# Hybrid decoder block on one core: right-hand tiles moved by 32 bytes, stores and loads moved between the SP and ACT queues, first, FFN-entry and last steps reordered

## The chip, the cores and the metric

The kernel runs on one core of one Trainium2 chip. The metric is the device time of one execution in microseconds (us). Of the kernel before, three runs are known: 1540.65, 1542.43 and 1542.45 us, median 1542.43. One further execution was profiled; the views quoted below are of it.

The engines: PE (TensorE) multiplies matrices, DVE (VectorE) and ACT (ScalarE) work element by element, POOL (GpSimd) too, and SP issues DMAs. Each engine takes its own instructions in the order in which they stand in the program. A DMA is issued by SP or by ACT, and its issue is an instruction of that engine like any other: if it has to wait, whatever stands behind it waits too.

## The reference

One decoder layer, 1024 positions by 1024 channels, fp32. Two branches, stick-breaking attention (8 heads of 64) and an HGRN2 recurrence (4 heads of 128), are merged by sigmoid gates and projected; a SwiGLU FFN with 2816 hidden channels follows.

```python
proj = rms_norm(x, norm1_g) @ w_in          # 1024 -> 5632
q_sb, k_sb, v_sb, q_hg, f_hg, i_hg, g_hg, gate_sb, gate_hg = split_cols(proj, IN_SIZES)
y_sb = stick_breaking_attention(q, k, v) @ w_branch[:512]
y_hg = hgrn2_mixer(q_hg, f_hg, i_hg, g_hg, lb, norm_g) @ w_branch[512:]
mixed = jax.nn.sigmoid(gate_sb) * y_sb + jax.nn.sigmoid(gate_hg) * y_hg
h = x + mixed @ w_out
hn = rms_norm(h, norm2_g)
out = h + (jax.nn.silu(hn @ w_gate) * (hn @ w_up)) @ w_down
```

## The kernel before, in words

**Operands.** Everything is kept transposed: 128 channels on the partitions, positions along the row, in halves of 512 (`hs(h)`). Each fp32 operand is split into a rounded part and a rest (`split`, L233: a cast on ACT for the first, a subtraction on DVE for the second), and each product is three matmuls of 128x512: hi·hi, hi·lo, lo·hi (`mm3` L297, `prod` L911, and L1060 to L1064). In the profile's names a matmul is `out<-moving,stationary`.

**Stages.** (1) Up to about 700 us: the input projection, attention and HGRN2, written as a list of operations that a planner (`Plan`, L74) puts in an order at build time; in the profile all of these have the line L182. (2) 700 to 785: the branch outputs times `wb` (L794 to L818). (3) 785 to 880: `w_out`, the residual sum `xx`, its store to the scratch tensor `h_d` (L860), and the operands `fop` of the FFN (L832 to L887). (4) 880 to 1320: gate and up, eleven pairs p of row blocks, each as a Winograd product of 2x2 blocks with seven sub-products numbered 1 to 7 (`winograd`, L961); the seven right-hand sums of each activation pair go to the scratch tensor `act_d` (L1008, L1017), those of `wd` to `wd_d`. (5) From 1320: the down projection, seven sub-products o in the order 1, 2, 6, 7, 4, 5, 3, each eleven pairs p of one `ra` (weights) and one `rb` (activations) tile, four banks d of 128 output rows (L1035 to L1079).

**Start.** ACT's first instruction is the load of its function table (L205). SP issues `vt<-vec` and then, in the planner's order, the eight x tiles `aa<-xT` of the first half with four weight tiles `kb<-wi` between them (L451 to L461). POOL makes the `oh` of each `kb`, DVE its `ol`; ACT makes the `ah` of each x tile, DVE its `al`.

**Queues.** Apart from the 32 `sig_d` stores, all DMAs are issued by SP in program order, so a load stands behind the stores written ahead of it. In stage 3 a chunk is one (k, h) of 24 matmuls; SP's load of the next `xx` stands behind the store of the last one. At the passage from stage 4 to 5 SP has the five stores of the last `act_d`, the loads of the pairs p = 4 to 10 of o = 1, 14 loads of `hb<-h_d`, and then the loads of o = 2; two further `hb` loads stand ahead of the stores. Pairs p = 0 to 3 of o = 1 (`early`, L1038) are loaded into other pools ahead of that. ACT has the casts `ah<-ra`, `bh<-rb` in order of p, and behind those of o = 1 four copies `acc<-f`, which wait for PE to end o = 1.

**FFN entry.** `winograd(..., begin=channel_sums)` runs once, for p = 0: sub-products 1, 5 and 6 over k = 0 to 2, then their k = 3 (whose operands are the last that stage 3 makes), then `begin()`, which sums the channels of `rr` (the squares that POOL adds up at L870), and only then ACT's copy `p1<-x` and DVE's `c[:, 1] = y + p1`, for which sub-product 7 waits.

**Addresses.** Pools are laid out from the left end of a partition's memory or, with `side="right"`, from the right end. In the built program every tile that PE streams from a left-hand pool (`xn`, `mx`, the `bh` and `bl` of stage 5) starts at a multiple of 64 bytes. The tiles of the right-hand pools start 32 bytes past such a multiple: among them the moving operands of stage 2 (`oh`, `ol` of `opool`, L786), all `fh`, `fl` of stage 4 (`fpool`, L824), and `khl` of the attention scores.

Of the kernel before, what the change touches and what calls it, by code (L numbers as in the profile page):

```python
# [10 lines left out]
F32 = mybir.dt.float32  # L11
# [8 lines left out]
P = 128  # L20
# [9 lines left out]
FILL = ["GgGGaifq", "gGaGfiqGG", "gaGGGiqGfGG", "gGGG"]  # L30
# [172 lines left out]
def hybrid_block(ctx: ExitStack, tc, xT, wi, wb, wo, wg, wu, wd, vec, outT):  # L203
    nc = tc.nc
    nc.scalar.preload_act_table_set("natural_log_exp_and_others")  # L205

# [19 lines left out]
    nc.sync.dma_start(vt, vec)  # L226
# [17 lines left out]

    rst = ExitStack()
# [47 lines left out]

    def hs(h):
        return slice(h * HALF, (h + 1) * HALF)
# [25 lines left out]
    xn = a_set(xst.enter_context(tc.tile_pool(name="xnp", bufs=1)))  # L321
    pre = ExitStack()
# [22 lines left out]
    st1 = ExitStack()  # L345
# [3 lines left out]
    hgp = st1.enter_context(tc.tile_pool(name="hgp", bufs=1, reuse_waits="tile"))  # L349
# [211 lines left out]

    COL = {"q": 0, "k": 4, "v": 8, "hq": 12, "hf": 16, "hi": 20, "hg": 24, "G": 28}
# [182 lines left out]
    fill = [("q", 0), ("k", 0), ("v", 0), ("hf", 0), ("hq", 0), ("hi", 0)]  # L745
# [85 lines left out]
    with tc.tile_pool(name="wot", bufs=4, reuse_waits="tile") as ot_:  # L831
        seq = [0, 4, 1, 5, 2, 6, 3, 7]  # L832
        wq = [get_w(wo[seq.pop(0)])]
        for i in range(4):
# [14 lines left out]
            for e in range(2):  # L849
# [4 lines left out]
                for h in range(2):  # L854
# [5 lines left out]
                    nc.sync.dma_start(h_d[k][:, hs(h)], xx)  # L860
# [6 lines left out]
                    else:  # L867
                        sq = tmp("sq")
                        nc.scalar.activation(sq, xx, AF.Square)
                        nc.gpsimd.tensor_tensor(rr[h], rr[h], sq, op=ALU.add)  # L870
# [65 lines left out]
    with ExitStack() as sta:  # L936
# [24 lines left out]
        def winograd(a, c, begin=None):  # L961
# [3 lines left out]
            if begin:  # L965
                for ks in ((0, 1, 2), (3,)):
                    for o, bank in ((1, x), (5, z), (6, y)):
                        prod(bank, a[o], fop[o], True, ks)
                begin()
                nc.scalar.copy(p1, x)  # L970
# [8 lines left out]
            prod(x, a[2], fop[2], False)  # L979
# [9 lines left out]
        for p in range(NP):  # L989
# [18 lines left out]
            nc.sync.dma_start(act_d[p][:, :4 * HALF], c.rearrange("p b t -> p (b t)"))  # L1008
# [7 lines left out]
            for b, t in ((4, n7), (5, n6), (6, n5), (7, n4)):  # L1016
                nc.sync.dma_start(act_d[p][:, b * HALF:(b + 1) * HALF], t)  # L1017
# [15 lines left out]
          5: [(d + 4, 1) for d in range(4)], 3: [(d, 1) for d in range(4)]}  # L1033
    bank = [None] * 4
    for o in DOWN:  # L1035
        first = o in (1, 6, 5)
        for p in range(NP):
            early = o == 1 and p < 4  # L1038
            wp, tags = bp, btags = dB, ("ah", "al")
            btags = ("bh", "bl")  # L1040
            if early:

                rp = wpool if p < 2 else preB
                raw = rp.tile([P, 1024], F32, tag="w", bufs=2, name="w32")
                ra, rb = raw[:, :512], raw[:, 512:]
                if p < 3:
                    wp = bp = rp
                    tags = btags = ("oh", "ol") if p < 2 else ("ds", "ds")
            else:
                ra = dB.tile([P, HALF], F32, tag="ra", name="ra")  # L1050
                rb = dB.tile([P, HALF], F32, tag="rb", name="rb")
            nc.sync.dma_start(ra, LEFT[o](p))
            nc.sync.dma_start(rb, blk(act_d[p], RIGHT[o]))
            hi, lo = split(ra, wp, tags)
            bh, bl = split(rb, bp, btags)
            for d in range(4):
                if first and p == 0:
                    bank[d] = fb()
                ws = slice(d * P, (d + 1) * P)
                nc.tensor.matmul(bank[d], hi[:, ws], bh, start=first and p == 0, stop=False,  # L1060
                                 skip_group_check=True)
                nc.tensor.matmul(bank[d], hi[:, ws], bl, start=False, stop=False,  # L1062
                                 skip_group_check=True)
                nc.tensor.matmul(bank[d], lo[:, ws], bh, start=False, stop=p == NP - 1,  # L1064
                                 skip_group_check=True)
        if o == 1:
            for k, h in ([(d, 0) for d in range(4)] + [(d, 1) for d in range(8)]
                         + [(d, 0) for d in range(4, 8)]):
                nc.sync.dma_start(hb[k][:, hs(h)], h_d[k][:, hs(h)])
            for d in range(4):  # L1070
                nc.scalar.copy(acc1[d], bank[d])
            continue
        for d, (k, h) in enumerate(TO[o]):
            t = hb[k][:, hs(h)]
            if o in (6, 7, 4):
                nc.vector.tensor_tensor(t, t, acc1[d], op=ALU.add)
            nc.vector.tensor_tensor(t, bank[d], t, op=ALU.add)
            if o in (2, 4, 5, 3):
                nc.sync.dma_start(outT[k][:, hs(h)], t)  # L1079
# [48 lines left out]
```

## Time and profile before

| What | Number |
| --- | --- |
| median of three runs | 1542.43 us (1540.65 to 1542.45) |
| the profiled execution, its own time | 1541.46 us |
| its span, first to last instruction | 1539.7 us |
| mean granted TensorE clock | 0.997 |
| DMA traffic | 188.5 MB, 122 GB/s over the span |
| DMA queue of SP (q1) / of ACT (q10) | 178.8 MB / 8.4 MB |

How the views are read: in the view of the stretches, a row gives the stretch, its length, then for each engine busy time and, in parentheses, how many instructions touched the stretch, the granted clock, the share of time the 16 DMA engines were busy, and GB/s. In the waits, a row gives who waited for whom, the sum, how often, and the longest. In the timeline, a row gives start, duration, engine, line, operation, `out<-in`, how many were merged, and in brackets the engine's idle time before it and what ended it. A matmul's end in the trace is modelled, so the pitch of matmuls is taken from how many start in a stretch. The stage borders above are read from the timeline.

### The profile page before, as it was taken

What the parts mean: (1) busy time and instruction counts of PE and PEld (TensorE: products, weight loads), DVE (VectorE), ACT (ScalarE), POOL (GpSimd) and SP (SyncE); (2) the same over time, 40 slices, a digit from 0 to 9 for tenths busy, and PEclk for the clock granted to TensorE, in tenths of its full rate; (3) what the DMA queues carried; (4) which work ended last, traced back from release to release, by engine and by line L of the source; (5) the groups of instructions that cost most, each with busy time, mean ns of one, the idle gap of its engine ahead of it and who ended that gap; (6) DMA issues with size and microseconds to landing.
All of it is one profiled execution on the core that took longest, in us unless ns stands there. A gap on an engine that the chain in (4) does not pass through costs nothing.

```text
span 1539.7 us, 20478 instructions
## 1 busy us (share of the span) xinstructions
PE 1515.8 (98%) x7213; PEld 1242.1 (81%) x7213; DVE 1184.3 (77%) x2046; ACT 800.4 (52%) x1503; POOL 178.8 (12%) x202
## 2 busy tenths in 40 slices
PE   8999999999999999999999989999999999999999
PEld 6788888888888888888888868778778888778887
DVE  8899679988898768965567798888877777475553
ACT  7866778678768778454333352233333333254442
POOL 4211111111111101114412200000000000000000
PEclk9999999999999999999999999999999999999999
DMA  5111211111111121245334455666633332787672
GB/s 178 41 43 44 76 33 42 59 39 52 50 52 41 59 69 48 71 160 201 125 107 133 139 163 205 217 211 208 213 136 110 105 105 94 270 274 220 193 220 92
DMA packets 78407, 188.53 MB, mean 122 GB/s; under 512 B 9056, under 2 KB 11104, under 8 KB 76896
## 3 DMA queue, kind: packets, MB, share of 16 engines
q1 hardware_dynamic: 73696, 178.83, 35.5%
q10 hardware_dynamic: 4608, 8.39, 1.5%
q8 instruction: 57, 0.93, 0.3%
q14 instruction: 46, 0.38, 0.1%
HBM read 131.61 MB, written 55.57 MB: 122 GB/s over the span
## 4 chain that ended last, share of the span: by engine, by line
PE 73%; DVE 11%; DMA 6%; ACT 4%; issue 4%; POOL 1%; SPq 1%; DVEq 0%; POOLq 0%; ACTq 0%
PE f L916 25%; PE pj L182 23%; PE ms L182 8%; PE f L1062 4%; PE f L1064 4%; PE f L1060 4%; PE z L182 2%; DMA xx<-xT 2%; DVE ol L238 1%; ACT aa L182 1%; DMA rb<-act_d 1%; POOL s L805 1%; DMA s<-sig_d 1%; DVE aa L182 1%; DVE tail L182 1%
## 5 line engine op out<-in xcount | busy, mean ns | idle before, releaser
L182 PE MATMUL pj<-ah,oh 128*128 128x512 f32 x704 | 286.7, 407 | 2.0 <-POOL oh L182 2.0
L182 PE MATMUL pj<-ah,ol 128*128 128x512 f32 x704 | 277.3, 394 | 0.9 <-DVE ol L182 0.9
L182 PE MATMUL pj<-al,oh 128*128 128x512 f32 x704 | 276.0, 392 | 0.0
L916 PE MATMUL f<-fh,oh 128*128 128x512 f32 x616 | 244.0, 396 | 3.4 <-ACT p L970 1.7
L916 PE MATMUL f<-fl,oh 128*128 128x512 f32 x616 | 243.4, 395 | 0.7 <-DVE fl L846 0.7
L916 PE MATMUL f<-fh,ol 128*128 128x512 f32 x616 | 243.2, 395 | 0.6 <-DVE ol L238 0.6
L237 ACT CAST oh<-w 128x512 fp32r<-128x512 f32 x168 | 102.1, 620 | 175.2 <-PE f L916 137.9
L182 PEld LDWEIGHTS pj<-ah,ol 128*128 128x128 f32 x704 | 132.6, 188 | 31.6 <-DVE ol L182 2.1
L182 PEld LDWEIGHTS pj<-ah,oh 128*128 128x128 f32 x704 | 133.1, 189 | 25.3 <-POOL oh L182 2.9
L182 PEld LDWEIGHTS pj<-al,oh 128*128 128x128 f32 x704 | 133.2, 189 | 22.9 <-issue 0.5
L916 PEld LDWEIGHTS f<-fh,oh 128*128 128x128 f32 x616 | 115.4, 187 | 34.3 <-ACT p L970 2.1
L916 PEld LDWEIGHTS f<-fh,ol 128*128 128x128 f32 x616 | 115.4, 187 | 29.1 <-DVE ol L238 1.0
L916 PEld LDWEIGHTS f<-fl,oh 128*128 128x128 f32 x616 | 115.5, 187 | 29.0 <-DVE fl L846 1.0
L238 DVE TENSOR_TENSOR ol<-w,oh 128x512 fp32r<-128x512 f32 x168 | 114.7, 690 | 30.0 <-ACT oh L237 29.8
L1062 PE MATMUL f<-bl,ah 128*128 128x512 f32 x296 | 117.0, 395 | 1.3 <-DVE bl L238 1.3
L1060 PE MATMUL f<-bh,ah 128*128 128x512 f32 x296 | 114.6, 391 | 3.7 <-ACT bh L237 3.7
L182 DVE TENSOR_TENSOR_SCAN aa<-aa,ww 128x128 f32<-128x128 f32 (+3 forms) x96 | 92.3, 975 | 33.4 <-ACT aa L182 23.8
L182 POOL TENSOR_SCALAR oh<-w 128x512 fp32r<-128x512 f32 x84 | 70.9, 844 | 394.0 <-PE pj L182 348.6
L1064 PE MATMUL f<-bh,al 128*128 128x512 f32 x296 | 116.6, 394 | 0.0
L238 DVE TENSOR_TENSOR al<-ra,ah 128x512 fp32r<-128x512 f32 x73 | 50.4, 690 | 72.0 <-ACT ah L237 71.9
L237 ACT CAST ah<-ra 128x512 fp32r<-128x512 f32 x73 | 45.5, 623 | 101.8 <-PE f L1062 93.7
L182 ACT ACTIVATE aa<-aa 128x512 f32<-128x512 f32 (+3 forms) x128 | 69.1, 552 | 4.9 <-DVE aa L182 4.0
(273 smaller groups left out, 2996.7 us busy)
## 6 DMA issues: line engine op xcount, KB each, us to landing
w<-wi SPq DMA_DIRECT2D x42, 512.0 KB, 3.6
rb<-act_d SPq DMA_DIRECT2D x73, 256.0 KB, 4.1
w<-wg SPq DMA_DIRECT2D x22, 512.0 KB, 3.9
w<-wu SPq DMA_DIRECT2D x22, 512.0 KB, 4.1
w<-wd SPq DMA_DIRECT2D x22, 512.0 KB, 6.8
wd_d<-ds SPq DMA_DIRECT2D x44, 256.0 KB, 5.4
act_d<-c SPq DMA_DIRECT2D x11, 1024.0 KB, 3.9
act_d<-bs SPq DMA_DIRECT2D x44, 256.0 KB, 3.5
```

The lines of the kernel that those rows point to most:

```text
L182: fn(*[a.real() if isinstance(a, View) else a for a in args], **{k: v.real() if isinstance(v, View) else v for k, v in kw.items()})
L237: pin(nc.scalar.copy(hi, src))
L238: pin(nc.vector.tensor_tensor(lo, src, hi.bitcast(F32), op=ALU.subtract))
L805: nc.gpsimd.tensor_tensor(s[:, hs(h)], s[:, hs(h)], rr1[h], op=ALU.mult)
L916: nc.tensor.matmul(out, a[i][:, ws], bl[k][j], start=start and k == 0 and i + j == 0, stop=k == 3 and i == 1, skip_group_check=True)
L1060: nc.tensor.matmul(bank[d], hi[:, ws], bh, start=first and p == 0, stop=False, skip_group_check=True)
L1062: nc.tensor.matmul(bank[d], hi[:, ws], bl, start=False, stop=False, skip_group_check=True)
L1064: nc.tensor.matmul(bank[d], lo[:, ws], bh, start=False, stop=p == NP - 1, skip_group_check=True)
```

## The change

It has nine parts. (a) A tile `edge` of 32 bytes is put at the right end ahead of all right-hand pools; in the built program every right-hand tile then starts at a multiple of 64 bytes. (b) `vt` and the four `kb` tiles are loaded by ACT, ahead of its table load; SP loads x alone. The planner now sees the `kb` tiles as present from the start. (c) One filler projection G changes places in the planner's list. (d) The `h_d` stores of stage 3 are issued by ACT. (e) The 14 sums of `rr` go from POOL to DVE. (f) In the first Winograd product sub-product 1 and its copy `p1` come first, sub-product 2 moves ahead of the last k of sub-product 6. (g) The last pair's `act_d` stores are issued by ACT. (h) The `hb` loads are issued by ACT, two behind each pair p >= 3 of o = 1. (i) In the last sub-product the last three pairs are run bank by bank, so that each bank ends, is summed and stored ahead of the next.

```diff
-FILL = ["GgGGaifq", "gGaGfiqGG", "gaGGGiqGfGG", "gGGG"]
+FILL = ["GgGGaifq", "gGaGfiqGG", "gGaGGiqGfGG", "gGGG"]
...
-    nc.scalar.preload_act_table_set("natural_log_exp_and_others")
...
-    nc.sync.dma_start(vt, vec)
+    nc.scalar.dma_start(vt, vec)
...
+    edge = ctx.enter_context(tc.tile_pool(name="edge", bufs=1, side="right"))
+    nc.gpsimd.memset(edge.tile([P, 8], F32, name="edge"), 0.0)
     rst = ExitStack()
...
+    first_w = []
+    for i in range(2):
+        for n, v in fill_cols[:2]:
+            t = hgp.tile([P, HALF], F32, tag="kb", bufs=4, name="kb")
+            nc.scalar.dma_start(t, wi[COL[n] + v][:, hs(i)])
+            first_w.append(t)
+    nc.scalar.preload_act_table_set("natural_log_exp_and_others")
...
-                n, v = fill[u]
-                w = new("kb")
-                load(w, wi[COL[n] + v][:, hs(i)], 256)
-                ws[u].append(split_w(w))
+                t = first_w[2 * i + u]
+                plan.ring("kb", 4)
+                ws[u].append(split_w(Buf("kb", lambda t=t: t)))
...
-                    nc.sync.dma_start(h_d[k][:, hs(h)], xx)
+                    nc.scalar.dma_start(h_d[k][:, hs(h)], xx)
...
-                        nc.gpsimd.tensor_tensor(rr[h], rr[h], sq, op=ALU.add)
+                        nc.vector.tensor_tensor(rr[h], rr[h], sq, op=ALU.add)
...
             if begin:
-                for ks in ((0, 1, 2), (3,)):
-                    for o, bank in ((1, x), (5, z), (6, y)):
-                        prod(bank, a[o], fop[o], True, ks)
+                prod(x, a[1], fop[1], True)
+                nc.scalar.copy(p1, x)
+                prod(z, a[5], fop[5], True)
+                prod(y, a[6], fop[6], True, range(3))
+                prod(x, a[2], fop[2], False)
+                prod(y, a[6], fop[6], True, (3,))
                 begin()
-                nc.scalar.copy(p1, x)
                 nc.vector.tensor_tensor(c[:, 1], y, p1, op=ALU.add)
...
             prod(y, a[7], fop[7], False)
-            prod(x, a[2], fop[2], False)
+            if not begin:
+                prod(x, a[2], fop[2], False)
...
-            nc.sync.dma_start(act_d[p][:, :4 * HALF], c.rearrange("p b t -> p (b t)"))
+            store = nc.scalar.dma_start if p == NP - 1 else nc.sync.dma_start
+            store(act_d[p][:, :4 * HALF], c.rearrange("p b t -> p (b t)"))
...
-                nc.sync.dma_start(act_d[p][:, b * HALF:(b + 1) * HALF], t)
+                store(act_d[p][:, b * HALF:(b + 1) * HALF], t)
...
+            if o == 1 and p >= 3:
+                for k, h in HB[2 * p - 6:2 * p - 4]:
+                    nc.scalar.dma_start(hb[k][:, hs(h)], h_d[k][:, hs(h)])
...
+    rest = [(p, operands(o, p)) for p in range(NP - LAST, NP)]
+    for d in range(4):
+        for p, ops in rest:
+            step(d, p, ops, False)
+        finish(o, d)
```

The functions `operands`, `step` and `finish` of the last piece hold the former loop bodies: the two loads with their splits, the three matmuls of one bank, and the sum into `hb` with its store.

**DVE at the start of the program.** `al` is the rest of an x tile, `ol` that of a weight tile, `tail` a sum of squares, `mk` a mask. Before:

```order
L292 TENSOR_SCALAR nomlb<-omlb 128x4
L182 SCALAR_TENSOR_TENSOR al_152<-aa,vt,ah_151 128x512
L182 TENSOR_TENSOR ol<-kb,oh 128x512
L182 SCALAR_TENSOR_TENSOR al_154<-aa,vt,ah_153 128x512
L182 TENSOR_TENSOR tail<-tail,ww 128x512
L182 TENSOR_TENSOR ol<-kb,oh 128x512
L182 SCALAR_TENSOR_TENSOR al_156<-aa,vt,ah_155 128x512
```

At the same place of the program as changed:

```order
L293 TENSOR_SCALAR nomlb<-omlb 128x4
L182 TENSOR_TENSOR ol<-kb,oh 128x512 x4
L182 SCALAR_TENSOR_TENSOR al_156<-aa,vt,ah_155 128x512
L182 COPY mk_242<-tmp 128x256
L182 SCALAR_TENSOR_TENSOR al_158<-aa,vt,ah_157 128x512
L182 SCALAR_TENSOR_TENSOR al_160<-aa,vt,ah_159 128x512
```

All four `ol<-kb` have moved ahead of the first `al`; PE's second matmul reads that `al` in both programs.

**ACT and SP at the passage from stage 4 to 5.** `w_12667` and `w_12672` are the raw tile of an early pair, `hb` the residual. ACT before:

```order
L237 CAST oh<-w_12303 128x512
L237 CAST oh<-w_12301 128x512
L237 CAST ah<-w_12667 128x512
L237 CAST bh<-w_12667 128x512
L237 CAST ah<-ra 128x512
L237 CAST bh<-rb 128x512
```

ACT of the program as changed:

```order
L235 CAST oh<-w_12308 128x512
L235 CAST oh<-w_12306 128x512
L1093 DMA hb_12587<-h_d_144 128x512
L1093 DMA hb_12588<-h_d_145 128x512
L1021 DMA act_d_132<-c 128x2048
L1030 DMA act_d_132<-bs 128x512 x4
L235 CAST ah<-w_12672 128x512
L235 CAST bh<-w_12672 128x512
L1093 DMA hb_12589<-h_d_146 128x512
L235 CAST ah<-ra 128x512
L235 CAST bh<-rb 128x512
```

SP before, from the loads of the early pairs on:

```order
L1052 DMA w_12621<-wd 128x512
L1053 DMA w_12621<-act_d_119 128x512
L1069 DMA hb_12582<-h_d_140 128x512
L1069 DMA hb_12583<-h_d_141 128x512
L1008 DMA act_d_128<-c 128x2048
L1017 DMA act_d_128<-bs 128x512 x4
L1052 DMA ra<-wd 128x512
L1053 DMA rb<-act_d_122 128x512
```

SP of the program as changed:

```order
L1066 DMA w_12626<-wd 128x512
L1067 DMA w_12626<-act_d_123 128x512
L1066 DMA ra<-wd 128x512
L1067 DMA rb<-act_d_126 128x512
L1066 DMA ra<-wd 128x512
L1067 DMA rb<-act_d_127 128x512
```

The `ra`, `rb` loads now follow the early pairs on SP with no store between, and ACT's casts from `w_12672` on stand behind five stores.

**DVE at the FFN entry.** The sum that sub-product 7 waits for is `g<-f,p`. Before:

```order
L846 TENSOR_TENSOR fl<-yy,fh 128x512
L238 TENSOR_TENSOR ol<-w_9155,oh 128x512
L238 TENSOR_TENSOR ol<-w_9157,oh 128x512
L907 TENSOR_TENSOR w_9155<-w_9155,s_9163 128x512
L900 TENSOR_TENSOR s_9201<-w_9195 128x512
L971 TENSOR_TENSOR g<-f,p_9233 128x512
```

The program as changed:

```order
L911 TENSOR_TENSOR w_9198<-s_9206,w_9198 128x512
L934 TENSOR_TENSOR parts<-rr_8385,parts 128x512
L951 TENSOR_TENSOR ds<-w_9359 128x512
L236 TENSOR_TENSOR ol<-w_9198,oh 128x512
L236 TENSOR_TENSOR ol<-w_9200,oh 128x512
L236 TENSOR_TENSOR ol<-w_9160,oh 128x512
L982 TENSOR_TENSOR g<-f,p_9238 128x512
```

From the last `xx<-pj,xx` of stage 3 to this sum it is 18 places in the program before and 23 in the changed one; the splits of the up weights (`w_9198`, `w_9200`) and a `ds` have moved ahead of it.

More of the change, by code (lines that the diff above doesn't have):

```diff
@@ L744, in hybrid_block @@
     ng = 0
[L745 removed]
+    fill = list(fill_cols)
     for u, seq in enumerate(FILL):
@@ L1035, in hybrid_block @@
     for o in DOWN:
         first = o in (1, 6, 5)
[L1037 to L1055, printed above, removed]
+        final = o == DOWN[-1]
@@ L1056, in hybrid_block @@
+        for p in range(NP - LAST if final else NP):
+            ops = operands(o, p)
+            if o == 1 and p >= 3:
+                for k, h in HB[2 * p - 6:2 * p - 4]:
+                    nc.scalar.dma_start(hb[k][:, hs(h)], h_d[k][:, hs(h)])
             for d in range(4):
@@ L1058, in hybrid_block @@
                     bank[d] = fb()
[L1059 to L1065, printed above, removed]
+                step(d, p, ops, first and p == 0)
         if o == 1:
-            for k, h in ([(d, 0) for d in range(4)] + [(d, 1) for d in range(8)]
-                         + [(d, 0) for d in range(4, 8)]):
-                nc.sync.dma_start(hb[k][:, hs(h)], h_d[k][:, hs(h)])
             for d in range(4):
                 nc.scalar.copy(acc1[d], bank[d])
[L1072 to L1079, printed above, removed]
+        elif not final:
+            for d in range(4):
+                finish(o, d)
+    rest = [(p, operands(o, p)) for p in range(NP - LAST, NP)]
+    for d in range(4):
+        for p, ops in rest:
+            step(d, p, ops, False)
+        finish(o, d)
 def _layout(inputs):
```

39 lines of the change are left out of this document (36 added, 3 removed).

## The prediction

> **What bounds the kernel now.** I read the page's head and chain first, then PE's waits, then the stretches.
>
> ```profile
> span 1539.7 us, 20478 instructions
> PE 1515.8 (98%) x7213; PEld 1242.1 (81%) x7213; DVE 1184.3 (77%) x2046; ACT 800.4 (52%) x1503; POOL 178.8 (12%) x202
> ```
>
> PE is busy for 1515.8 of 1539.7 us. So there are only two sources of time: the 24 us in which PE does nothing, and the pace of its matmuls. PE's waits in stages 4 and 5:
>
> ```profile
> PE f L1060 <- ACT bh L237: 3.7, 2, 2.0
> ...
> PE f L916 <- ACT p L970: 1.7, 1, 1.7
> PE f L1062 <- DVE bl L238: 1.3, 1, 1.3
> PE f L916 <- ACT fh L845: 1.1, 1, 1.1
> PE f L916 <- DVE fl L846: 0.7, 1, 0.7
> PE f L916 <- DVE ol L238: 0.6, 1, 0.6
> PE f L916 <- DVE g L971: 0.5, 1, 0.5
> ```
>
> L916 waits for 1.7 + 1.1 + 0.7 + 0.6 + 0.5 = 4.6 us, all at the FFN entry (880 to 896); L1060 and L1062 for 3.7 + 1.3 = 5.0 us at the passage from stage 4 to 5. The pace is read from four stretches in which PE has no gap and streams 512 columns throughout:
>
> ```profile
> 705.00:780.00 75.00, 75.00 (x323) 60.26 (x322) 45.75 (x64) 27.19 (x39) 34.09 (x25) 1.00 0.43 140
> 790.00:875.00 85.00, 85.00 (x377) 70.32 (x376) 61.81 (x88) 31.28 (x54) 16.47 (x12) 1.00 0.42 134
> 897.00:1320.00 423.00, 422.85 (x1810) 338.62 (x1810) 348.59 (x560) 134.23 (x222) 0.00 (x0) 1.00 0.46 157
> 1359.50:1530.00 170.50, 170.50 (x754) 141.21 (x753) 94.06 (x149) 67.95 (x120) 0.00 (x0) 1.00 0.64 199
> ```
>
> A matmul's record lasts longer than the pitch, so each count holds two that began before the stretch. The pitch is 75.00/321 = 0.2336, 85.00/375 = 0.2267, 423.00/1808 = 0.2340 and 170.50/752 = 0.2267 us, all at a granted clock of 1.00. The first and third stretch stream tiles from right-hand pools (32 bytes past a multiple of 64), the other two tiles from left-hand pools (at the multiple).
>
> **(a) The edge tile.** It adds one POOL memset at the start, beside other work. If the 32 bytes make the difference of pitch, every matmul that streams from the right falls to 0.2267.
>
> ```profile
> L916 PE MATMUL f<-fh,oh 128*128 128x512 f32 x616 | 244.0, 396 | 3.4 <-ACT p L970 1.7
> ```
>
> There are three such groups (hi·hi, hi·lo, lo·hi), so 1848 matmuls: 1848 x (0.2340 - 0.2267) = 13.5 us. Stage 2 has 384: 384 x 0.0069 = 2.6. The attention scores from `khl` are few and short; I give them nothing. The sum is **-16**. Other explanations of the pitch hardly fit: DVE is busy for 348.59/423 = 82% in the third stretch, but 61.81/85 = 73% in the second, which is fast, and 45.75/75 = 61% in the first, which is slow; the DMA share is highest (0.64) in a fast one. The bounds are 0, if something else in those stages sets the pitch, and -17.
>
> That row of four pitches stands against a rule of the Trainium skill ("SBUF — State Buffer", its table of facts), which has cachelines of 16 bytes: a start at 32 and one at 64 are both multiples, so by it the term would be 0. This is rival A below; the trace so far speaks against it.
>
> **(g, h) The passage.** Time, duration, engine, and in brackets the idle time before:
>
> ```profile
> 1323.47 0.61 SPq L1052 DMA_DIRECT2D ra<-wd  x1
> 1327.38 0.62 ACT L237 CAST ah<-ra 128x512 fp32r<-128x512 f32 x1 [7.54 <-DMA ra<-wd]
> 1329.91 0.62 ACT L237 CAST bh<-rb 128x512 fp32r<-128x512 f32 x1 [1.91 <-DMA rb<-act_d]
> 1330.58 1.50 PE L1060 MATMUL f<-bh,ah 128*128 128x512 f32 x4 [1.95 <-ACT bh L237]
> 1333.27 9.11 SPq L1069 DMA_DIRECT2D hb<-h_d  x14
> 1349.53 2.62 ACT L1071 COPY acc<-f 128x512 f32<-128x512 f32 x4 [10.83 <-PE f L1064]
> ...
> 1330.50:1335.50 5.00, 4.92 (x15) 3.91 (x16) 4.91 (x8) 4.56 (x9) 0.00 (x0) 0.66 1.05 394
> 1353.00:1359.50 6.50, 4.97 (x15) 3.73 (x16) 6.50 (x12) 5.93 (x13) 0.00 (x0) 0.74 0.64 204
> ```
>
> Before, the first `ra` is issued at 1323.47, behind the `act_d` stores; its cast comes at 1327.38, that of `rb` at 1329.91, and PE waits. Then `hb` holds SP from 1333.27 to 1342.38, ahead of the loads of o = 2, and PE waits a second time at 1353. Each wait is followed by a stretch of lower clock: 5.00 x (1 - 0.66) = 1.7 us and 6.50 x (1 - 0.74) = 1.7. In the changed order no store and no `hb` stands ahead of the `ra` loads on SP; they wait only for free tiles, and those are free long before 1320, since the early pairs use other pools. So both waits and both cold stretches go: 5.0 + 1.7 + 1.7 = **-8.4**. What is late next is ACT's cast of the last early pair (`w_12672`), which now stands behind two `hb` and five `act_d` issues. I put the last `bs` at about 1322, and the pair is needed three pairs of 12 matmuls after the start of stage 5, 36 x 0.23 = 8 us later. An issue costs 0.61 us by the `ra` row, or 9.11/14 = 0.65 by the `hb` row: 7 x 0.65 = 4.6 us of ACT, which fits, barely. `hb` is not used before DVE's sums behind o = 1, after 1349. Bounds: -8.4, and +4 if the casts of that pair and the next two come late by what `rb` was late before (2 us each).
>
> **(d, e, f) The FFN entry.**
>
> ```profile
> 878.64 0.32 SPq L860 DMA_DIRECT2D h_d<-xx  x1
> 879.05 0.38 SPq L856 DMA_DIRECT2D xx<-xT  x1
> 882.94 0.69 DVE L859 TENSOR_TENSOR xx<-pj,xx 128x512 f32<-128x512 f32 x1 [1.09 <-DMA xx<-xT]
> 894.81 0.68 DVE L971 TENSOR_TENSOR g<-f,p 128x512 f32<-128x512 f32 x1
> ...
> L870 POOL TENSOR_TENSOR rr<-rr,sq 128x512 f32<-128x512 f32 x14 | 19.7, 1409 | 82.8 <-ACT sq L869 82.8
> L846 DVE TENSOR_TENSOR fl<-yy,fh 128x512 fp32r<-128x512 f32 x18 | 16.6, 924 | 5.4 <-ACT fh L845 5.0
> ```
>
> The last `xx` load, issued at 879.05 behind the store of the last chunk, keeps DVE's last residual sum until 882.94. With the stores on ACT it can come about 3 us earlier, at 880. But the sum for sub-product 7 then stands 23 places on instead of 18: from 882.94 to 894.81, 18 places took 11.87 us, 0.66 each, so it starts at 880 + 23 x 0.62 = 894.3 with the shorter pieces among them, 0.5 earlier than before. PE has one block of 4 matmuls more to do by then (sub-product 2 but for nothing, instead of the last k of 5), so it waits some 0.5 less there. But DVE is as late as before, and its splits of the other weights can hold PE at new places. I take **-0.5**. Bounds: -4.6 (all waits go), +2.5 (one new wait of 2 us, with part of a cold stretch behind it, by the passage's prices).
>
> The 14 sums of `rr` cost POOL 1.41 us each; on DVE, by the 0.69 of the `xx` row, 14 x 0.69 = 9.7 us. Most of that is covered: PE has no gap in 790 to 875, where DVE is busy 73% (83% with these). And `fl` takes 0.924 there against 0.69 for like operations, so while POOL works beside it DVE seems slower; 18 x 0.23 = 4 us and more come back. Net 0. If that cover is gone, the 23 places above grow; that is in the +2.5.
>
> **(b) The start.**
>
> ```profile
> 11.68 0.81 POOL L182 TENSOR_SCALAR oh<-kb 128x512 fp32r<-128x512 f32 x1 [0.22 <-DMA kb<-wi]
> ...
> 5.80 0.68 DVE L182 TENSOR_TENSOR ol<-kb,oh 128x512 fp32r<-128x512 f32 x1
> 7.95 0.75 DVE L182 SCALAR_TENSOR_TENSOR al<-aa,vt,ah 128x512 fp32r<-128x512 f32 x1 [1.47 <-ACT ah L182]
> ...
> 13.88 0.39 PE L182 MATMUL pj<-al,oh 128*128 128x512 f32 x1
> ...
> 0.80 1.28 ACT L205 ACT_TABLE_LOAD   x1 [0.80 <-PEq L1110]
> ...
> 6.50:14.00 7.50, 5.08 (x13) 3.49 (x13) 6.05 (x8) 6.30 (x11) 4.31 (x8) 0.77 1.00 360
> ```
>
> The fourth `kb` landed just ahead of POOL's cast at 11.68. In the changed order all four `ol<-kb` precede the first `al`, for which PE's second matmul waits. If that `kb` lands as late as before, `oh` ends at 12.5, `ol` at 13.2, `al` at 13.9; PE then starts where it had done 13 matmuls before (the stretch's count). That is 13 x 0.23 = 3.0 us of work, and a second cold start of 7.50 x (1 - 0.77) = 1.7, less some 0.8 of small waits after 9 us that go: +3.9. But the four weights are now issued by about 3 us instead of 5.7, and share the DMA engines (busy share 1.00) with as many x tiles: at 360 GB/s, by the same row, a tile of 256 KB takes 0.73 us, so it may land up to 2 us earlier, for +1.9. I take **+2.5**, nearer to the earlier landing. The table load (1.28) now stands behind five issues, so ACT's first `ah` is about 1 us later, hidden behind the weights. Bounds: -0.5 and +4.8.
>
> DMAs of several engines share the same 16 DMA engines and a second queue saves only issue time, says the Trainium skill ("DMA: Bandwidth & Descriptors", "Issuing engines are not separate DMA queues"). The share of 1.00 in the last row agrees; by that rule alone the later landing holds, and the sum would be 1.4 us worse.
>
> **(c, i) Filler and end.**
>
> ```profile
> 60.00:680.00 620.00, 616.50 (x3366) 518.33 (x3366) 520.16 (x1005) 445.59 (x913) 91.57 (x113) 1.00 0.17 52
> ...
> 1533.99 2.73 DVE L1077 TENSOR_TENSOR hb<-f,hb 128x512 f32<-128x512 f32 x4 [12.55 <-PE f L1064]
> 1534.70 2.37 SPq L1079 DMA_DIRECT2D outT<-hb  x4
> 1535.60 0.39 PE L1064 MATMUL f<-bh,al 128*128 128x512 f32 x1
> ```
>
> Where G stands can change only the 620 - 616.50 = 3.5 us of gaps: **0**, bounds -3 and +3. At the end DVE's four sums begin at 1533.99, ahead of the last matmul at 1535.60: only the last sum and its store follow it, which stay: **0**.
>
> **Sum**: -16 - 8.4 - 0.5 + 2.5 = -22.4. The profiled execution took 1541.46 us; minus 22.4 gives 1519.1. The median shown (1542.43) is 1.0 above it, so I predict **1520.0**.
>
> **The rivals.**
> *A, the 32 bytes do nothing.* The pitch then belongs to the stages, for instance to DVE writing from the same pools. For it: the two slow stretches share no stage with the fast ones. Against it: the DVE and DMA shares above do not order as the pitches do. The time is 1520 + 16 = 1536.
> *B, the passage gives nothing.* ACT waits at its issues and the casts of `w_12672` come late, which opens a wait and a cold stretch in place of those removed. For it: the tight 4.6 us. Against it: three early pairs are cast before. 1520 + 8.4 = 1528.
> *C, slower.* In stage 3 ACT holds at each `h_d` store until DVE's sum is done, and its weight casts behind it come late, in each of 14 chunks. The last sum ended 882.94 + 0.69, over 4 us after the store of the chunk before it at 878.64. Casts run about one weight ahead (24 matmuls of 0.2267 = 5.4 us a chunk), which should cover it. It decides from 22.4/14 = 1.6 us of PE waiting in a chunk; at half of 4.2, 14 x 2.1 = 29, so 1549.
> *D, the moves cancel*: A's zero with a new FFN or start-up wait of 6 us beside the passage's gain: about 1542.
>
> **How the numbers follow.** Forecast 0.70, A 0.12, B 0.11, C 0.03, D 0.04. The forecast's own range follows from its bounds: down by 4.1 at the entry, 3.0 at the start and 3 by the filler, which seldom come together (the root of the squares is 6, with 1 to 2 more in (a)): 1512. Up it has 2 to 3 us from each of these, and B at 1528: 1529. A, C, D (0.19) lie above. 0.2%, about 3 us, is about what a measurement of this kernel tells from no change: faster 0.93 (forecast, A, B), same 0.04, slower 0.03.
>
> **What would show it.** (a) is right if 897 to 1320 has a pitch near 0.227, wrong at 0.234; (g, h) if L1060 and L1062 have no wait and the clock stays at 1.00 from 1305 to 1345; (d, e, f) by the waits of L916's successor; (b) by the start of PE's second matmul with real data, 12 to 14 us; C by PE waits between 785 and 880. A wait of over 2 us anywhere that pulls the clock down would break the sum.

## The result: 1554.8 us, slower by 0.9%

| What | Before | After |
| --- | --- | --- |
| median | 1541.54 us (1540.60 to 1542.45, 4 runs) | 1554.78 us (1553.79 to 1557.10, 4 runs) |
| ratio | | 1.0088, 95% interval 1.0071 to 1.0106 |
| span of the profiled execution | 1539.7 us | 1551.9 us |

The forecast was 1520.0 us with a range of 1512 to 1529, so both the sign and the size are wrong. The head of the page of the changed kernel:

```profile
span 1551.9 us, 20437 instructions
PE 1507.1 (97%) x7213; PEld 1241.5 (80%) x7213; DVE 1189.5 (77%) x2060; ACT 801.0 (52%) x1503; POOL 153.9 (10%) x189
```

PE has the same 7213 matmuls and is busy 8.7 us less, and yet the span is 12.2 us longer: the matmuls got faster, and the waits grew by more. PE's waits, the largest of the view (who waited for whom, sum, how often, longest):

```profile
PE pj L306 <- ACT oh L797: 8.7, 1, 8.7
PE f L925 <- ACT p L976: 5.7, 1, 5.7
PE pj L182 <- DVE al L182: 4.8, 1, 4.8
PE f L925 <- DVE g L987: 3.8, 5, 1.4
PE z L306 <- DVE t L823: 3.4, 4, 1.0
```

Of the five only the wait for `p` stood in the view of before, with 1.7 us. The waits of the passage (L1060 and L1062 then, L1074 now) are nearly gone. What that makes in time is seen best when PE's matmuls are counted in the order of their starts, since the stages have the same numbers of them in both programs. The table gives the time from one matmul's start to another's:

| Stretch (matmuls) | Before | After | Difference | Forecast |
| --- | --- | --- | --- | --- |
| start, to the 60th | 23.9 | 26.1 | +2.2 | +2.5 |
| rest of stage 1, to the 3600th | 662.4 | 668.9 | +6.5 | 0 |
| end of stage 1 and first two chunks of stage 2, to 3765 | 38.0 | 51.4 | +13.4 | -0.6 |
| rest of stage 2, to 4053 | 67.2 | 68.7 | +1.5 | -2.0 |
| stage 3, to 4437 | 87.1 | 87.0 | 0 | 0 |
| FFN entry: gate product of p = 0 and a little more, to 4609 | 46.0 | 47.8 | +1.8 | -1.8 |
| rest of stage 4, to 6289 | 393.0 | 386.1 | -6.9 | -12.2 |
| first two sub-products of stage 5, to 6553 | 68.7 | 62.4 | -6.3 | -8.4 |
| the rest | 153.5 | 153.5 | 0 | 0 |

The sum is +12.2, the difference of the spans. (In the last column the 16 us of the edge tile are spread over the stages that they were counted for.)

**Where the 13.4 us are.** SP around the end of stage 1, first before, then after:

```profile
675.76 0.33 SPq L182 DMA_DIRECT2D o_d<-tail  x1
676.18 12.78 SPq L785 DMA_DIRECT2D o<-o_d  x8
689.05 0.39 SPq L230 DMA_DIRECT2D w<-wb  x1
```

```profile
689.78 0.33 SPq L228 DMA_DIRECT2D w<-wb  x1
690.24 0.45 SPq L182 DMA_DIRECT2D o_d<-ot  x1
701.10 11.20 SPq L228 DMA_DIRECT2D w<-wb  x2
712.36 2.19 SPq L794 DMA_DIRECT2D o<-o_d  x4
```

Before, the eight loads `o<-o_d` follow the last store of `o_d` at once, 25 us ahead of stage 2. After, two loads of `wb` for later steps stand between them. Each waits for a free `w` tile, that is for the splits of a gate projection, and those come one gate projection apart: the first load goes out at 701.10, and the second ends at 701.10 + 11.20 = 712.30. Everything behind is held: `o` is issued at 712.36, 22 us after the last store. ACT shows the end of it:

```profile
711.74 0.33 ACTq L182 DMA_DIRECT2D sig_d<-tmp  x1
718.40 1.04 ACT L797 CAST oh<-o 128x1024 fp32r<-128x1024 f32 x1 [6.68 <-DMA o<-o_d]
```

PE starts stage 2 at 719.49 after 8.7 us of nothing. The two chunks behind it (48 matmuls each) take 13.9 and 13.0 us, where each took 11.2 before:

```profile
719.40:733.40 14.00, 13.65 (x49) 10.16 (x50) 10.40 (x9) 9.29 (x10) 1.43 (x1) 0.84 0.84 304
733.40:746.40 13.00, 11.47 (x50) 8.85 (x49) 7.90 (x9) 5.78 (x7) 13.00 (x10) 1.00 0.45 136
```

In the first, PE hardly waits, but its granted clock is 0.84, which is worth 14.00 x 0.16 = 2.2 us. In the second it waits twice for the products `t` of DVE (L822, L823), 1.5 us in all: `t` needs the sigmoids `s`, and the loads of `sig_d` for them stand behind those of `o` on SP, the first at 724.88.

**The FFN entry**, ACT and DVE of the changed kernel:

```profile
906.47 0.33 ACTq L869 DMA_DIRECT2D h_d<-xx  x1
906.84 0.63 ACT L878 ACTIVATE sq<-xx 128x512 f32<-128x512 f32 x1 [1.94 <-DVE xx L868]
907.38 0.60 ACT L235 CAST oh<-w 128x512 fp32r<-128x512 f32 x1
909.58 0.62 ACT L933 CAST parts<-rr 128x512 fp32r<-128x512 f32 x1 [1.59 <-DVE rr L879]
...
914.84 0.58 ACT L976 COPY p<-f 128x512 f32<-128x512 f32 x1
```

```profile
905.75 0.69 DVE L868 TENSOR_TENSOR xx<-pj,xx 128x512 f32<-128x512 f32 x1
906.47 0.48 DVE L871 TENSOR_SCALAR yy<-xx,vt 128x512 f32<-128x512 f32 x1
908.25 0.69 DVE L890 TENSOR_TENSOR t<-yy 128x512 f32<-128x512 f32 x1 [1.29 <-DMA h_d<-xx]
908.86 0.68 DVE L879 TENSOR_TENSOR rr<-rr,sq 128x512 f32<-128x512 f32 x1
```

The copy `p1` has its bank ready at about 905, but stands on ACT behind the last `h_d` store, `sq`, the cast of `parts` and eight more casts, and comes at 914.84. Sub-product 2, moved ahead, adds into the bank that it copies, so PE waits from 909.8 to 915.47. DVE in turn waits until 908.25 for an `h_d` store to land, because `t` takes over a tile that the store reads. DVE's sum `g<-f,p`, for which sub-product 7 waits, starts at 920.97, 18.8 us after the first matmul of the entry (902.15); before, it was 894.81 - 878.62 = 16.2 us after it.

**The pitch.** Stage 4 behind the first pairs, before and after (the view of the stretches):

```profile
1165.00:1315.00 150.00, 150.00 (x645) 120.47 (x643) 110.36 (x176) 45.22 (x75) 0.00 (x0) 1.00 0.31 105
```

```profile
1185.00:1335.00 150.00, 150.00 (x664) 124.20 (x663) 114.59 (x182) 45.51 (x76) 0.00 (x0) 1.00 0.33 113
```

With two matmuls off each count, 150/643 = 0.2333 has become 150/662 = 0.2266 us.

### The profile page after: what moved, and what is told of

Read it like the earlier page. It is cut to its first block, busy times and chain, and to the rows that moved or that the text cites. A ratio compares the mean times of both kernels' runs of the same rounds, so it can differ in the third digit from the quotient of the medians.

```text
span 1551.9 us, 20437 instructions
## 1 busy us (share of the span) xinstructions
PE 1507.1 (97%) x7213; PEld 1241.5 (80%) x7213; DVE 1189.5 (77%) x2060; ACT 801.0 (52%) x1503; POOL 153.9 (10%) x189
## 3 DMA queue, kind: packets, MB, share of 16 engines
q1 hardware_dynamic: 67648, 167.28, 33.1%
## 4 chain that ended last, share of the span: by engine, by line
PE 61%; DVE 18%; DMA 6%; ACT 6%; issue 4%; POOL 3%; ACTq 0%; SPq 0%; POOLq 0%; DVEq 0%
PE pj L182 18%; PE f L925 18%; PE f L1074 12%; PE ms L182 8%; ACT aa L182 2%; DVE aa L182 2%; POOL s L814 2%; DVE ol L236 2%; DMA w<-wu 2%; PE z L182 2%; DVE kb L182 1%; DMA s<-sig_d 1%; PE pj L306 1%; PE pj L308 1%; PE pj L307 1%
## 5 line engine op out<-in xcount | busy, mean ns | idle before, releaser
L925 PE MATMUL f<-fl,oh 128*128 128x512 f32 x616 | 240.1, 390 | 0.0
L1074 PE MATMUL f<-bl,ah 128*128 128x512 f32 x296 | 115.5, 390 | 0.6 <-DVE bl L236 0.6
L1074 PE MATMUL f<-bh,ah 128*128 128x512 f32 x296 | 115.0, 390 | 0.4 <-ACT acc L1100 0.2
L1074 PE MATMUL f<-bh,al 128*128 128x512 f32 x296 | 115.2, 389 | 0.0
L182 POOL TENSOR_SCALAR oh<-w 128x512 fp32r<-128x512 f32 x84 | 65.0, 774 | 401.4 <-PE pj L182 356.1
L182 ACT ACTIVATE ww<-ww 128x384 f32<-128x384 f32 (+3 forms) x96 | 49.5, 524 | 44.0 <-DVE ww L182 41.0
```

What stands on the lines that cost most here:

```text
L182: fn(*[a.real() if isinstance(a, View) else a for a in args], **{k: v.real() if isinstance(v, View) else v for k, v in kw.items()})
L925: nc.tensor.matmul(out, a[i][:, ws], bl[k][j], start=start and k == 0 and i + j == 0, stop=k == 3 and i == 1, skip_group_check=True)
L1074: nc.tensor.matmul(bank[d], l[:, ws], r, start=start and i == 0, stop=p == NP - 1 and i == 2, skip_group_check=True)
```

## The experiments

e4, e8 and e10 were measured four or five times; the time of each other experiment is that of one run. Runs of one kernel here lie up to 6 us apart, so small differences are read from the stretches between matmuls and not from the totals.

**First: what slowed stage 1 and held the loads of `o`?** The changed kernel opens the pool `hgp` ahead of `tmpp`, `stk` and `att`, so that the first weights can be loaded into it early. That moves all four. In the built programs the four `o32` tiles of stage 2, into which `o` is loaded, lie over these tiles of stage 1 (numbered by address; the fourth is the second to be loaded):

| `o32` tile | Before | After |
| --- | --- | --- |
| 1 to 3 | `att`: `aa`, `ww` | `hgp`: `xi`, `xg`, `dl`, `ql`, `bl` |
| 4 | `att`: `ww` | `hgp`: `ql`, `state`; `tmpp`: `tmp` (the source of the `sig_d` stores) |

e1 puts the old places back, with the rest as changed:

```diff
+    tmpp = st1.enter_context(tc.tile_pool(name="tmpp", bufs=1, reuse_waits="tile"))
+    stk = st1.enter_context(tc.tile_pool(name="stk", bufs=1, reuse_waits="tile"))
+    att = st1.enter_context(tc.tile_pool(name="att", bufs=1, reuse_waits="tile"))
     hgp = st1.enter_context(tc.tile_pool(name="hgp", bufs=1, reuse_waits="tile"))
...
-    tmpp = st1.enter_context(tc.tile_pool(name="tmpp", bufs=1, reuse_waits="tile"))
-    stk = st1.enter_context(tc.tile_pool(name="stk", bufs=1, reuse_waits="tile"))
-    att = st1.enter_context(tc.tile_pool(name="att", bufs=1, reuse_waits="tile"))
```

> The changed kernel, with tmpp, stk and att opened ahead of hgp as before, so that the four o32 tiles of stage 2 lie over tiles of att again and not over hgp's and tmpp's tmp. Theory L (the new place of hgp in memory put the o loads behind the last gate projection): PE's wait of 8.7 us before the first matmul of stage 2 goes, the two chunks behind it fall from 13.9 and 13.0 to 10.9 to 11.3 us, the last three of stage 2 from 12.1 to about 11; in all 1554.8 - 13 to 17 = 1538 to 1542. Rival P (the stores of o_d land late because the planner ends stage 1 in another order): the wait stays over 6 us and the time at 1552 to 1555.

Measured: 1544.0 us. The wait is gone, and the two chunks behind it take 11.3 and 10.9 us. The last three of stage 2 stayed at 36.2 us in all, so the time is 2 us above what was expected. Theory L holds for the wait.

e2 is e1 with an empty step, one without an instruction, added to the planner's list where the load of each `kb` had stood:

```diff
-                ws[u].append(split_w(Buf("kb", lambda t=t: t)))
+                n, v = fill[u]
+                w = Buf("kb", lambda t=t: t)
+                last_load[0] = plan.op("D", 256 / 350, [(lambda *a: None, (w, wi[COL[n] + v][:, hs(i)]), {})],
+                                       1, (last_load[0],))
+                ws[u].append(split_w(w))
```

> As e1, and the planner still counts the four kb loads as work of SP's queue at their old places, though ACT issues them; the list of fillers stays as changed. Theory K (the planner, told that the kb tiles are there from the start, made an order of stage 1 with more waits): the 6.5 us that stage 1 lost behind its 60th matmul fall to under 2, 1533 to 1537 in all. Rival C (the filler that changed places did it): they stay at 5 to 7, and the time at that of e1 within 2.

Measured: 1530.05 us, below what was expected. The 60th to the 3600th matmul take 664.2 us, 1.8 above before (after: 668.9). The 60th comes at 24.1 us, where it was 23.9 before and 26.1 after. Stage 2 runs at 10.9 us a chunk to its end. Theory K holds. Against e1, from which e2 differs by this step alone, the start is 2.1 us shorter, the rest of stage 1 is 4.8 shorter (669.0 there), and so is the rest of stage 2 by 4.6 (70.0 to 65.4). So the planner's new order cost nearly all of the 2.2 at the start, 4.7 us of the 6.5, and, with the old places of the pools, the last chunks of stage 2.

> The changed kernel with the old list of fillers. Rival C: the 6.5 us of stage 1 go, 1548. Theory K with L: stage 1 keeps 4 to 8 of them and the wait before stage 2 stays at 7 to 10, so 1552 to 1557.

e3 has the one line of FILL as before. Measured: 1560.5 us, above both forecasts: stage 1 is 4.9 us slower still (673.8), and the wait before stage 2 remains. So the new list of fillers helps the changed plan, and rival C falls. Beside the old order it may cost 1 to 2 us: stage 1 takes 663.2 to 664.2 in e2, e5, e6 and e7, and 661.9 in e10 below. But e10 also has the start of before, so the list's part is not shown.

e9 makes the sharpest test of L: the kernel before, with the one line that opens `hgp` put ahead of the other three pools, and nothing else.

```diff
+    hgp = st1.enter_context(tc.tile_pool(name="hgp", bufs=1, reuse_waits="tile"))
     tmpp = st1.enter_context(tc.tile_pool(name="tmpp", bufs=1, reuse_waits="tile"))
     stk = st1.enter_context(tc.tile_pool(name="stk", bufs=1, reuse_waits="tile"))
     att = st1.enter_context(tc.tile_pool(name="att", bufs=1, reuse_waits="tile"))
-    hgp = st1.enter_context(tc.tile_pool(name="hgp", bufs=1, reuse_waits="tile"))
```

> The kernel before with one edit: hgp is opened ahead of tmpp, stk and att, so that stage 2's o32 tiles lie over hgp and tmpp. Theory L: that alone brings the wait before stage 2, 6 to 10 us, two slow chunks behind it and the last of stage 2 at 12.1 us each; stage 1 is as before within 1; 1552 to 1558. Rival: it needs the later end of the changed plan; 1540 to 1544.

Measured: 1558.6 us. Stage 1 is within 1.0 of before. Its waits and SP:

```profile
PE pj L302 <- ACT oh L788: 8.0, 1, 8.0
```

```profile
676.66 0.33 SPq L182 DMA_DIRECT2D o_d<-tail  x1
677.09 0.38 SPq L856 DMA_DIRECT2D xx<-xT  x1
682.50 22.03 SPq L230 DMA_DIRECT2D w<-wb  x3
704.63 1.94 SPq L785 DMA_DIRECT2D o<-o_d  x4
```

The last `o_d` store is issued at 676.66, as early as before, and still three loads of `wb` now hold SP until 704.63. One line that computes nothing costs 18 us in one run. Of these, 14.0 lie between the 3600th matmul and the end of stage 2 (12.2 in the stretch in which the changed kernel lost 13.4, and 1.8 behind it); the rest is scattered over start, stage 4 and passage.

That the order of SP turned is shown. But the new addresses hold the loads in any order: in the built program the second `o` load waits for the landing of the last but one `sig_d` store, whose source `tmp` lies under its tile. In e9 that store is issued at 698.24, and such a store lands some 2 us later, so this load could not go before about 700 (in the kernel before it went at 676.66); the loads of `wb` add the time up to 705.13. Why the build's scheduler turned the order (this later date may be the reason) is only argued.

**Second: the edge tile.** e4 is the kernel before with the two lines of `edge`.

> The kernel before with the edge tile alone. Theory A1 (each right-hand matmul 7.3 ns shorter, nothing else): stage 4 shorter by 12 to 13.5 us, stage 2 by 2 to 2.6, 1526 in all. Theory A2 (what feeds PE takes over): stage 2 gains under 1, since its loop of loads, POOL, ACT and DVE repeats every 12.07 us whatever PE does, and the first five pairs of stage 4 gain nothing, since DVE holds them; 1531 to 1534. Rival A of the prediction: pitch stays at 0.234, 1541.

Measured: 1530.15 us, ratio 0.9940 (0.9918 to 0.9961). Both theories have a part. The pitch falls, and stage 2 gains its 2.4 us: its loop has slack enough when it starts in time. Stage 4 as a whole gains 8.4 us, not 12 to 13.5. e4's built program has the instructions of the kernel before in the same order, with one `memset` more. The two stretches of e4, late pairs and early pairs:

```profile
1155.00:1305.00 150.00, 150.00 (x663) 124.22 (x662) 114.33 (x182) 46.12 (x77) 0.00 (x0) 1.00 0.31 109
925.00:1115.00 190.00, 187.03 (x822) 153.59 (x821) 166.73 (x270) 59.23 (x100) 0.00 (x0) 1.00 0.64 215
```

In the late pairs PE has no gap, at 150/661 = 0.2269 us, and DVE is busy 76%. In the early ones PE waits 3 us and DVE is busy 88%, with 270/190 = 1.42 instructions per us against 182/150 = 1.21.

e12 is the kernel of e10 (below) without what makes the early pairs heavier for DVE; it leaves the sums of `wd` out and stores pieces of `wd` in their place:

```diff
-            s7, s6, s5, s3 = (preB.tile([P, HALF], F32, tag="ds", bufs=4, name="ds")
-                              for _ in range(4))
-            sub(s7, a11, a21)
-            sub(s6, a22, s7)
-            nc.vector.tensor_tensor(s5, s6, a11, op=ALU.add)
-            sub(s3, a12, s6)
-            for b, t in enumerate((s7, s6, s5, s3)):
+            for b, t in enumerate((a11, a21, a12, a22)):
```

> The kernel of e10 with the four sums ds of each pair left out (wd_d gets pieces of wd in their place). Theory D (DVE, which does eight or nine ds in each of the pairs 0 to 5 and none later, bounds them): those pairs take 38.1 us each as the later ones do, instead of 38.3 to 39.3, 3 to 4 us less in all. Rival (the order of ACT's casts bounds them): no change over 1 us.

Measured: 1526.9 us, 4.7 above e10, so the total went the other way. Pairs 1 and 2 take 85.0 us together (e10: 77.0), since the loads and stores of `wd` now run ahead on SP and the next gate weights come late:

```profile
939.78 0.62 ACT L237 CAST oh<-w 128x512 fp32r<-128x512 f32 x1 [11.20 <-DMA w<-wg]
```

Behind that, pairs 3 and 4 take 76.6 us and 5 and 6 take 76.2, where e10 has 78.0 and 78.3; 76.2 is what PE needs. These four pairs fit theory D. The total leaves it short of settled.

**Third: the FFN entry**, from e2, whose first 48 matmuls there take 18.3 us (before: 16.9). e5 puts the old order of the first product back, with `p1` behind the sums:

> The kernel of e2 with the first Winograd product in the order of before (sub-products 1, 5, 6 over three k, then their last k, then the sums, and only then the copy p1). Theory O (sub-product 2, put ahead, makes PE wait for ACT's copy p1, which stands behind twelve casts): the wait of 5.7 us for p goes or falls under 2, the 48 matmuls from the entry on fall from 18.3 to 16.5 to 17 us, 1528 to 1529 in all. Rival V (DVE's sums are the bound at the entry, whatever the order): the wait turns up at fh, ol or g and the 48 matmuls take 18 to 19 us; 1530.

Measured: 1527.9 us, but the 48 matmuls take 19.0 us. The wait for `p` fell to 1.2, and `parts` (3.1), `fh` (1.8) and `fl` (0.7) took its place. To the 172nd matmul the old order takes 48.6 us, against 47.9 in e2. That is rival V; the lower total comes from other stretches, mostly the passage (61.8 us against 63.5). e6 has one word changed:

```diff
-                    nc.scalar.dma_start(h_d[k][:, hs(h)], xx)
+                    nc.sync.dma_start(h_d[k][:, hs(h)], xx)
```

> The kernel of e2 with the h_d stores of stage 3 on SP. Theory H (on ACT a store is issued later and lands over 2 us after the last xx, and DVE's next sum, which takes over a tile, waits 1.4 us for it): that wait of DVE goes, the copy p1 is 1 to 1.5 us earlier, 48 matmuls in 17 to 17.5, 1529. Rival: the load of the last xx comes later behind SP's stores, as before, and takes it back; 18.3 to 19 us, 1530 to 1531.

Measured: 1522.2 us, a much larger gain than expected. The 48 matmuls take 12.9 us instead of 18.3, and up to the 172nd the gain is 5.0. DVE and ACT of e6:

```profile
879.99 0.69 DVE L872 TENSOR_TENSOR xx<-pj,xx 128x512 f32<-128x512 f32 x1 [0.34 <-DMA xx<-xT]
880.72 0.49 DVE L875 TENSOR_SCALAR yy<-xx,vt 128x512 f32<-128x512 f32 x1
881.24 0.69 DVE L894 TENSOR_TENSOR t<-yy 128x512 f32<-128x512 f32 x1
```

```profile
887.30 0.58 ACT L980 COPY p<-f 128x512 f32<-128x512 f32 x1
```

`t` follows with no wait, and the copy comes 9.6 us after the entry (877.70); in e2 it came 12.7 after it. PE's wait for `p` is 1.7 us instead of 5.7, and no stretch of low clock follows it:

```profile
877.00:900.00 23.00, 17.30 (x70) 13.82 (x69) 21.33 (x36) 13.66 (x23) 0.00 (x0) 0.85 0.48 165
877.00:900.00 23.00, 20.59 (x89) 16.20 (x88) 21.50 (x37) 16.60 (x26) 0.00 (x0) 1.00 0.71 221
```

(e2 first, then e6.) Of the 7.9 us between the two totals, 5.0 are gained here, to the 172nd matmul; the others lie in stretches that the edit does not touch.

> The kernel of e2 with the sums of rr on POOL. If POOL's work slows DVE (fl takes 0.92 us beside it and 0.69 without), DVE's sums of fl go back to 0.85 to 0.95 us, and the entry takes as long as in e2 or longer, 18.3 to 20 us for 48 matmuls. If the 14 sums are simply work taken from DVE, the entry is shorter by 1 to 2 us.

e7 has the sums of `rr` on POOL (`nc.gpsimd` for `nc.vector`). Measured: 1526.8 us. `fl<-yy` takes 899 ns on average in stage 3 and 686 in e2, so POOL's work does slow DVE. But the 48 matmuls take 14.9 us, and the entry, to the 172nd matmul, is 2.9 us shorter than in e2 (45.0 against 47.9), so the sums were also work taken from DVE at the place where it is short.

**Fourth: the passage, and what is worth keeping.**

> The kernel before with the edge tile, the last act_d stores on ACT and the hb loads on ACT, and nothing else of the change. If the parts add up as the traces say (edge -10 as in e4, the passage 68.9 us for 264 matmuls of which 63 to 64 are left in the changed kernel, so -5 to -6), the time is 1524 to 1526, and the ratio 0.990. Rival (the passage's gain in the changed kernel came from the later times of its loads): 1528 to 1531.

e8, with the edits (a), (g) and (h) alone, measured 1527.3 us, ratio 0.9912 (0.9889 to 0.9936), between the two forecasts; its passage takes 62.2 us. The gain there (6.5) is thus independent of the rest. Stage 4, in which e8 has the same work as e4, took 2.9 us more in the profiled execution (433.5 against 430.6), which took some of it back. e10 keeps (a) and (e) to (i), without (b), (c) and (d):

> The changed kernel without its start (b), its filler list (c) and its h_d stores on ACT (d): edge, sums of rr on DVE, the new order at the FFN entry, act_d stores and hb loads on ACT, the last steps bank by bank. If the ledgers of e6 and e8 add up (e6 less the 2.1 us that stage 1 and 0.6 that the start took there), 1519 to 1521. If the entry's gain in e6 hung on the changed start, 1523 to 1527.

Measured: 1522.2 us (1520.4 to 1524.7), ratio 0.9875 (0.9859 to 0.9892): it beats both kernels, 1.2 us above what was expected. e11 is e10 with the `hb` loads on SP again, ahead of the loads of o = 2 in the source:

> The kernel of e10 with the hb loads on SP ahead of the loads of o = 2, as before. Theory S (each of the two moves takes away one of the passage's two waits): the first 132 matmuls of stage 5 take 31 to 33 us, the next 132 go from 30.4 back to 33 to 34.4, and the time is 3 to 4 us above e10. Rival (the stores alone made both): both stay, and the time is that of e10 within 1.

Measured: 1523.9 us beside e10's profiled execution of 1524.7, with 32.8 and 29.9 us for the two stretches (e10: 33.1 and 30.4). So the rival holds, as far as one run shows it: the stores of (g) made the gain, and (h) added nothing. SP of e11 shows why:

```profile
1304.67 8.41 SPq L1092 DMA_DIRECT2D hb<-h_d  x3
...
1322.64 4.31 SPq L1092 DMA_DIRECT2D hb<-h_d  x7
```

With no store in the way, the scheduler places nine of the sixteen `hb` loads early (the last three are shown) and seven behind the loads of o = 1, where they hold SP for 4.3 us instead of the 9.11 us of fourteen.

## Why the prediction was wrong

**(c, i) "Where G stands can change only the 620 - 616.50 = 3.5 us of gaps: 0".** Here and in (b) lie the steps that failed most. Stage 1's gaps were taken as a ceiling, and stage 1 was put at 0 behind its start; it came out 6.5 us longer. The list with G was not the cause (with the old list it is 4.9 longer still, e3). The order of stage 1 was remade: (b) told the planner that the `kb` tiles are there from the start, and it moved what it issues everywhere behind. With a placeholder for the loads 4.7 of the 6.5 us went (e2). And the step looked at no queue beyond stage 1: the `o` loads lie on SP between it and stage 2, and no term of the sum was about them.

**(b) The start** was priced as a start only, and there it was right, mechanism included: +2.2 for +2.5, with PE's second matmul at 12.39 us. The price came from the four `ol` ahead of the first `al`; with the old plan, e2 has them apart and loses 0.2. Loading on ACT gained nothing by itself (e2's 60th matmul at 24.1 us, 23.9 before). The Trainium skill ("DMA: Bandwidth & Descriptors", "Issuing engines are not separate DMA queues") has DMAs of all issuing engines run on the same 16 DMA engines, so that a second issuer saves only issue time, and these starts agree. But (b) also moved a pool, and the pool moved stage 2's tiles. In the stretch at the border that was 13.4 us here, and 12.2 with e9's single line; with the old places of the pools it went (e1). This is the missing mechanism of the prediction, named by none of its rivals: the sum put -0.6 there.

**The latent loop of stage 2.** The forecast had -2.6 for its matmuls. From the third to the fifth chunk they took 10.9 us each, while the loads were ahead, and then 12:

```profile
778.22 5.62 POOL L814 TENSOR_TENSOR s<-s,rr 128x512 f32<-128x512 f32 x4 [6.44 <-DMA s<-sig_d]
790.12 2.83 POOL L814 TENSOR_TENSOR s<-s,rr 128x512 f32<-128x512 f32 x2 [6.28 <-DMA s<-sig_d]
...
802.38 2.75 POOL L814 TENSOR_TENSOR s<-s,rr 128x512 f32<-128x512 f32 x2 [6.36 <-DMA s<-sig_d]
```

Load, POOL, ACT's sigmoid, DVE and the next load repeat every (802.38 - 778.22)/2 = 12.1 us, longer than PE's chunk. Before, the loads of `sig_d` began 12 us ahead of stage 2, and that lead seems to have hidden it: with 9.3 us of lead (e1) it shows from the fifth chunk on, with 12.5 us (e2) not at all. The changed kernel starts stage 2 with no lead (first load at 724.88, start at 719.49).

**(a) The edge tile** was right in mechanism: rival A fell with e4. The size was off. The pitch of 0.2340 came from a stretch that held DVE's small waits; the late pairs alone give 0.2333. And the first pairs, where DVE is busier than the 82% that was quoted as an average, had little room for a faster PE: the second to sixth pair took 196.9 us before, 195.7 in the changed kernel and 194.5 in e4, where five late pairs take 190.5. So they gained about a quarter to a half of what the late ones did. That DVE is what held them is likely and not settled (e12). By the Trainium skill ("SBUF — State Buffer", table of facts, cachelines of 16 bytes) the 32 bytes should make no difference; e4's 0.2269 decides against that reading.

**(d, e, f) The entry**: "With the stores on ACT it can come about 3 us earlier" had the sign wrong. DVE's last sum `xx` comes 3.5 us after the first matmul of the entry with the stores on ACT (e2), and 2.3 after it with them on SP (e6). On ACT the store waits for DVE's sum and holds `sq` behind it, and its landing holds DVE's `t`. The step also counted DVE's places alone, and what PE met was ACT's copy `p1`. DVE's sum for sub-product 7, forecast 0.5 us earlier, came 2.6 later. The sums (e) were put at 0 and cost the entry 2.9 us beside the stores on ACT (e7). Rival C named the store on ACT, but looked for the price in 14 chunks, where stage 3 lost nothing; it was paid once, at the end, 5.0 us (e6). What the new order (f) is worth is only partly shown: 0.7 us with the stores on ACT (e5). With them on SP, (e) and (f) together shorten the entry from 44.9 us (e4) to 43.7 (e10), and no run has (f) alone.

**(g, h) The passage** was right in place and sign: -6.3 for -8.4, though by (g) alone. What is left is seen in the stretch where the last small waits lie:

```profile
1358.00:1370.00 12.00, 11.04 (x43) 7.62 (x43) 6.10 (x10) 6.45 (x13) 0.00 (x0) 1.00 1.05 385
```

The 16 DMA engines are full there (1.05, 385 GB/s), so it is likely that moving issues does no more; no run tests it. Rival B's late casts did not come. The tail (i) was 0, as said.

**The chances.** 3% for slower was far too little: the plan and the addresses were open, and the sum treated their 680 us as fixed. Without the planner's and the pool's part the changed kernel takes 1530.05 us (e2), about 10 above the forecast: the entry, the rest of stage 4 and the passage gave less than the sum had.

## What to carry to other kernels

A pool that is opened earlier moves the addresses of the pools after it, and with them what later tiles must wait for and how the build orders the loads. So compare each queue's order, and what its loads wait for, at every stage border, also far from the edit. A store belongs on the queue whose engine has nothing waiting behind it. And before a faster matmul is multiplied by its count, look for the stretches in which another engine is near 90%, and for loops that only their lead hides.

## What the runs showed of the hardware

The start of PE's moving tile, 32 bytes past a multiple of 64, costs 0.2333 - 0.2269 = 6.4 ns in each 128x512 matmul (e4, with the edge tile alone). POOL beside DVE slows DVE: `fl<-yy` took 924 ns before, 899 in e7, and 686 in e2, where POOL no longer adds `rr`. And a wait costs more than itself: after the 8.7 us ahead of stage 2 the granted clock is 0.84 for 14 us, and after the 5.7 us at the entry,

```profile
900.00:942.00 42.00, 35.35 (x149) 28.27 (x148) 38.88 (x65) 24.25 (x39) 0.00 (x0) 0.96 0.48 157
```

the granted clock of the stretch is 0.96, 1.7 us of its 42, while the stretches shown without a long wait have 1.00.
